# Gathering rows with the one-hot slots as weights, two tiles' choices interleaved, and a shorter untaken branch in a two-layer encoder with a mixture of experts

## The chip, the cores and the metric

The kernel is one program on one core of a Trainium2 chip. The metric is device microseconds of that core for the whole program; lower is better.

## What is computed

The reference is a two-layer encoder over 512 tokens of width 1024 (float32). Each layer is a mixer (attention and recurrences) and then a mixture of experts: every token chooses one of 4 groups, two of the 8 experts in it, and gets the weighted sum of two experts' outputs. Each sub-layer ends in a layer norm. Cut to the part that the change touches:

```python
for i in range(DEPTH):                       # 2
    mix = mixer_i(x, ...)
    x = _layer_norm(ALPHA * x + mix, ln1_g[i], ln1_b[i])
    # mixture of experts
    grp = x @ w_grp + b_grp                  # 4 logits
    exp = (x @ w_exp + b_exp)                # 32 logits
    g_idx = argmax(grp); top_l, top_e = top_k(exp of that group, 2)
    gate = softmax(grp)[g_idx] * softmax(top_l)
    ffn = sum over the two experts e of gate_e * (silu(x @ w_gate[e]) * (x @ w_up[e])) @ w_down[e]
    x = _layer_norm(ALPHA * x + ffn, ln2_g[i], ln2_b[i])
```

The weights of the 32 experts are 201 MB a layer, and all of them are read.

## The kernel before, in words

Tokens lie in 4 tiles of 128 (`NT`). Every expert has 64 slots (`CAP`); two experts make a pair, so 16 pairs of 128 slots. A token's place among an expert's slots is counted by matmuls with a triangle and with ones (`moe_count`); the one-hot matrix `S` (token by slot) is a comparison of that place with 1..64 (`moe_slots`). If an expert has more tokens than slots, a general path (`moe_general`, inside `tc.If(over > 0)`) computes the layer without slots. With this input neither layer takes it, and no row of it is in the trace; the program still loads the flag `rover` on each engine, branches over the path, and lifts the semaphores that the path would have lifted.

`out_rest` is the seam between mixer and experts. For each tile t it finishes the output projection (`out`), adds the residual (`total`), normalizes (`norm`), transposes the tile (`turn`, 8 transposes on TensorE and two copies on ScalarE to `mxT`), computes the 36 logits (`logits`), picks group and experts (`choose`, 13 lines on VectorE that wait each for the one before), counts, places (`place`, which makes `S` for the first pair) and gathers the first pair's rows (`gather`). TensorE and VectorE run this stage in the order in which the code stands. Then come the slots of the second pair for all four tiles, the token numbers of the second pair (`moe_tokens`), the indirect DMA that fetches that pair's rows (`moe_fetch`, issued by GpSimd), two copies of the gathered rows to `xbuf`, and in `moe` the branch and the experts: `up(0, 0)` is the first matmul against expert weights.

In the gather before, the weights of each matmul are a 128 x 128 block of token rows and the 128 slots are the moving operand, so that the result is already transposed as `up` wants it:

```python
for j in range(KJ):          # 8
    self.mm(m["g"][:, j * P:(j + 1) * P], xv[:, j, :], S, ...)
```

Expert weights are loaded by SyncE in blocks of 1 MB (`expect_moe`) to 24 slots of 8 KB a partition (`big`), each as soon as a slot is free. While the seam runs, the slots fill up and no more loads can start until `up(0, 0)` frees the first two.

Of the kernel before, what the change touches and what calls it, by code (L numbers as in the profile page):

```python
# [77 lines left out]
class Kernel:  # L78
# [159 lines left out]
    def setup(self):  # L238
# [209 lines left out]
    def out_rest(self, pool, gbuf, m):  # L448
# [11 lines left out]
        def half_room():  # L460
# [7 lines left out]
            self.nc.gpsimd.memset(m["xr"], 0.0)  # L468
# [44 lines left out]
        def choose(t):  # L513
            self.moe_choose(m, pool, t, ps[t][1])
# [19 lines left out]
        with self.tc.manual_schedule(engines={mybir.EngineType.PE, mybir.EngineType.DVE}):  # L534
# [27 lines left out]
            choose(2)  # L562
            turn(3)
# [453 lines left out]
    def moe_choose(self, m, r, t, pl):  # L1017
# [3 lines left out]
        nc.vector.tensor_tensor(lg, pl, m["br"], op=OP.add)  # L1021
# [6 lines left out]
        def first_hot(o, v, mx, k, op):  # L1028

            fm = r.tile([P, 1], F32, name="fm", bufs=8)  # L1030
            nc.vector.tensor_reduce(mx, v, axis=AX.X, op=OP.max)
            nc.vector.scalar_tensor_tensor(o, v, mx, wt[:, 0:k], op0=OP.is_equal, op1=OP.mult, accum_out=fm)
            nc.vector.tensor_scalar(o, o, 2.0, fm, op0=OP.mult, op1=op)

        first_hot(og, lg[:, 0:4], m["gmx"][:, t:t + 1], NG, OP.is_le)

        nc.vector.scalar_tensor_tensor(grid(s), og[:, :, None].to_broadcast([P, NG, EPG]), -3.0e38, grid(lg[:, 4:36]), op0=OP.mult, op1=OP.add)
        A0, A1 = m["A0"][:, t, :], m["A1"][:, t, :]
        first_hot(A0, s, m["m12"][:, 0, t:t + 1], NE, OP.is_gt)
# [882 lines left out]
```

## Time and profile before

| | us |
|---|---|
| median of 3 runs (1594.83 to 1597.14) | 1596.24 |
| the profiled execution | 1594.33 |
| its span from first to last instruction | 1592.2 |
| TensorE busy in it | 1513.1 |
| VectorE busy | 692.0 |
| ScalarE busy | 440.2 |
| GpSimd busy | 188.0 |
| mean DMA rate | 292 GB/s |

The layers' seams lie at about 305 to 350 us and 1063 to 1107 us, the experts after them to about 815 and 1565 us. Rows from the trace give a start and a length in us from the span's start; PE is TensorE, PEld its weight loads, DVE VectorE, ACT ScalarE, POOL GpSimd, SP SyncE. A "q" behind an engine's name is its sequencer, which runs branches and waits.

### The profile page before, as it was taken

How to read it: one execution, taken by the hardware profiler on the slowest of the kernel's cores; microseconds unless marked ns; L12 is line 12 of the kernel's file. 1: busy time of each engine (PE TensorE's matmuls, PEld its weight loads, DVE VectorE, ACT ScalarE, POOL GpSimd, SP SyncE). 2: the span in 40 equal slices, each digit the busy share in tenths (PEclk: the TensorE clock that was granted, in tenths of full speed). 3: DMA queues.
4: the chain of work that ended last, by engine and by line, in shares of the span. 5: the costliest groups of instructions: out<-in, count | busy, mean ns of one | idle time of the engine just before them, and what ended most of it. 6: DMA issues, size and time to landing. Idle time of an engine off the chain costs nothing. (4 is left out here: it accounts for less than half of the span.)

```text
span 1592.2 us, 19865 instructions
## 1 busy us (share of the span) xinstructions
PE 1513.1 (95%) x7905; PEld 915.1 (57%) x7905; DVE 692.0 (43%) x1215; ACT 440.2 (28%) x770; POOL 188.0 (12%) x278
## 2 busy tenths in 40 slices
PE   7999999979999999999999899998999999999997
PEld 7888788764444444443358787677444444444333
DVE  4655655543334343343445544364333434333334
ACT  4455522012211211211235434511221121111122
POOL 3322211211000000010022200120000000001001
PEclk9999999979999999999999999997999999999999
DMA  8311133749999999999962120385999999999993
GB/s 236 107 54 54 54 133 106 298 164 398 421 419 419 421 421 419 420 420 421 419 246 94 54 75 32 123 338 186 396 420 420 419 421 421 419 419 420 421 420 137
DMA packets 106844, 465.20 MB, mean 292 GB/s; under 512 B 12972, under 2 KB 48268, under 8 KB 57456
## 3 DMA queue, kind: packets, MB, share of 16 engines
q1 hardware_dynamic: 98848, 444.86, 69.8%
q0 software_dynamic: 6160, 12.62, 2.3%
q10 hardware_dynamic: 1728, 6.29, 1.0%
q8 instruction: 67, 1.10, 0.3%
q14 instruction: 41, 0.34, 0.1%
HBM read 462.11 MB, written 9.44 MB: 296 GB/s over the span
## 5 line engine op out<-in xcount | busy, mean ns | idle before, releaser
L213 PE MATMUL pa<-big 128*64 128x512 f32 (+3 forms) x4168 | 838.6, 461 | 18.1 <-DMA big<-in_moe_w_up_dram 7.2
L213 PEld LDWEIGHTS pa<-big 128*128 128x128 f32 (+1 forms) x4168 | 453.0, 166 | 329.9 <-issue 278.5
L213 PE MATMUL pa<-big,hs 128*64 128x512 f32 x992 | 224.9, 592 | 0.0
L1205 DVE SCALAR_TENSOR_TENSOR big<-pa,rgate,big 64x512 fp32r<-64x512 f32 x120 | 90.0, 750 | 213.4 <-ACT big L1204 213.2
L213 PE MATMUL pb<-big 128*128 128x512 f32 (+2 forms) x640 | 173.9, 418 | 6.3 <-DVE big L1160 4.1
L1160 DVE SCALAR_TENSOR_TENSOR big<-big,pb 128x1024 f32<-128x1024 f32 x112 | 134.3, 1220 | 80.0 <-PE pb L213 79.7
L213 PEld LDWEIGHTS pa<-big,hs 128*64 128x64 f32 x992 | 72.6, 137 | 141.0 <-issue 136.1
L213 PEld LDWEIGHTS pb<-big 128*128 128x128 f32 x640 | 122.7, 217 | 51.0 <-issue 26.0
L1204 ACT ACTIVATE big<-pa,rgate 64x512 fp32r<-64x512 f32 x120 | 81.8, 682 | 219.0 <-PE pa L213 170.3
L1175 DVE TENSOR_TENSOR h<-pa,h 64x512 f32<-64x512 f32 x64 | 44.4, 694 | 216.2 <-ACT h L1174 216.2
L1174 ACT ACTIVATE h<-pa 64x512 f32<-64x512 f32 x64 | 37.6, 588 | 260.8 <-PE pa L213 260.8
L203 DVE TENSOR_TENSOR big<-big 128x2048 fp32r<-128x2048 f32 (+2 forms) x38 | 77.0, 2025 | 67.2 <-ACT big L203 49.5
L203 ACT CAST big<-big 128x2048 fp32r<-128x2048 f32 (+2 forms) x39 | 64.7, 1665 | 57.2 <-PE pa L213 23.1
L1139 POOL DMA_INDIRECT big<-x1d,ridx x30 | 31.7, 1058 | 368.4 <-DVE ridx L1113 255.8
L1148 ACT COPY big<-pb 128x1024 f32<-128x1024 f32 x30 | 30.4, 1012 | 127.7 <-PE pb L218 127.7
L1138 POOL MEMSET big<- 128x1024 f32 x28 | 26.6, 952 | 311.8 <-PE pb L218 311.7
L218 PEld LDWEIGHTS pa<-eye,h 64*128 64x128 f32 x256 | 35.4, 209 | 37.8 <-DVE big L1205 23.5
L213 PE MATMUL pb<-big,C 128*128 128x512 f32 x192 | 53.9, 412 | 2.5 <-DVE big L1160 2.5
L218 PE MATMUL pb<-eye,big 128*128 128x128 f32 x288 | 42.6, 288 | 12.4 <-DMA big<-in_x_dram 5.9
L218 PEld LDWEIGHTS pb<-eye,big 128*128 128x128 f32 x288 | 37.3, 195 | 18.5 <-issue 7.5
L1185 DVE COPY hs<-pa 128x256 f32<-128x256 f32 x64 | 27.0, 422 | 44.8 <-PE pa L218 44.7
L213 PEld LDWEIGHTS pb<-big,C 128*128 128x128 f32 x192 | 33.3, 188 | 19.4 <-issue 9.7
(312 smaller groups left out, 1200.5 us busy)
## 6 DMA issues: line engine op xcount, KB each, us to landing
big<-in_moe_w_gate_dram SPq DMA_DIRECT2D x128, 1024.0 KB, 19.8
big<-in_moe_w_up_dram SPq DMA_DIRECT2D x128, 1024.0 KB, 19.8
big<-in_moe_w_down_dram SPq DMA_DIRECT2D x128, 1024.0 KB, 19.8
big<-in_ev_w_in_dram SPq DMA_DIRECT2D x24, 512.0 KB, 5.6
big<-in_od_w_in_dram SPq DMA_DIRECT2D x7, 1024.0 KB, 6.8
big<-in_x_dram SPq DMA_DIRECT2D x8, 512.0 KB, 4.3
big<-in_ev_w_out_dram SPq DMA_DIRECT2D x4, 1024.0 KB, 4.9
x1d<-big ACTq DMA_DIRECT2D x8, 512.0 KB, 7.0
```

The lines of the kernel that those rows point to most:

```text
L203: ins = self.nc.scalar.copy(hi, src), (sub or self.nc.vector).tensor_tensor(lo, src, hi.bitcast(F32), op=OP.subtract)
L213: return self.nc.tensor.matmul(o, a, b, start=start, stop=stop, skip_group_check=True)
L218: self.nc.tensor.transpose(o, a, self.eye[s, s])
L1138: self.nc.gpsimd.memset(x, 0.0)
L1139: self.nc.gpsimd.indirect_dma_start(x, None, self.x1d[:, :], bass.IndirectOffsetOnAxis(m["idx"][:, pair:pair + 1], 0), bounds_check=T - 1, ...
L1148: self.nc.scalar.copy(xn, ps.rearrange("p (j n) -> p j n", j=KJ))
L1160: self.nc.vector.scalar_tensor_tensor(x, x, ALPHA if first else 1.0, ps, op0=OP.mult, op1=OP.add)
L1174: self.nc.scalar.activation(h, o[0:64], AF.Silu)
L1175: self.nc.vector.tensor_tensor(h, o[64:128], h, op=OP.mult)
L1185: self.nc.vector.tensor_copy(hs.rearrange("p j n -> p (j n)"), ps[:, 0:4 * CAP])
L1204: last = self.nc.scalar.activation(hi, src, AF.Copy, scale=g[a:a + 64])
L1205: self.nc.vector.scalar_tensor_tensor(yl[a:a + 64, s], src, g[a:a + 64], hi.bitcast(F32), op0=OP.mult, op1=OP.subtract)
```

## The change

- The gather uses `S` as weights and the token rows as moving operand: 2 matmuls of 512 columns a tile in place of 8 of 128. The result lies slot by feature, so after the branch two copies (one on ScalarE, one on VectorE) bring it to `xr` and `moe_features` transposes it (8 transposes, two copies).
- `choose(1, 2)` interleaves the 13 lines of two tiles. Its place, and those of `turn`, `logits` and `gather`, move.
- `place` makes the slots of both first pairs at once (256 columns); the token numbers and the fetch of pair 1 move behind the branch.
- `turn` writes all 8 transposes before its two copies; `mxT` gets a third buffer.
- `moe_general` is one loop over tiles in place of four copies of a loop body.
- A filler of 160 bytes a partition moves what is allocated behind it: in the built program every `big` slot starts 96 bytes past a multiple of 256 before, and at a multiple of 256 after.

```diff
+        c.tile([P, 40], F32, name="pad")
...
-            self.nc.gpsimd.memset(m["xr"], 0.0)
+            self.nc.gpsimd.memset(self.moe_fetched(m, 1), 0.0)
...
-            xT[t] = pool.tile([P, D], F32, name="mxT", bufs=2).rearrange("p (j n) -> p j n", j=KJ)
+            xT[t] = pool.tile([P, D], F32, name="mxT", bufs=3).rearrange("p (j n) -> p j n", j=KJ)
...
-        def choose(t):
-            self.moe_choose(m, pool, t, ps[t][1])
+        def choose(*ts):
+            for steps in zip(*[self.moe_choose(m, pool, t, ps[t][1]) for t in ts]):
+                for f in steps:
+                    f()
...
-            xv = res[t].rearrange("p (k j) -> p j k", j=KJ)
             S = m["S"][:, t, 0:2].bitcast(F32).rearrange("p e n -> p (e n)")
-            for j in range(KJ):
-                self.mm(m["g"][:, j * P:(j + 1) * P], xv[:, j, :], S, t == 0 and j % 4 == 0, t == NT - 1)
+            for hf in range(2):
+                s = slice(hf * 512, (hf + 1) * 512)
+                self.mm(m["g"][:, s], S, res[t][:, s], t == 0, t == NT - 1)
...
+            count(0)
             st = total(3)
+            place(0)
             logits(1)
-            count(0)
-            place(0)
             norm(3, st)
             turn(2)
-            choose(1)
+            gather(0)
             logits(2)
+            turn(3)
+            choose(1, 2)
             count(1)
             place(1)
-            gather(0)
-            choose(2)
-            turn(3)
+            logits(3)
             gather(1)
             count(2)
             place(2)
-            logits(3)
+            choose(3)
             gather(2)
-            choose(3)
             count(3)
-            pc = self.moe_fit(m)
-            place(3)
+            place(3, 1)
+            self.moe_fit(m)
             gather(3)
-            self.moe_fits(m, pc)
-            for t in range(NT):
-                self.moe_slots(m, t, 1)
-            z = self.pa()
-            self.moe_tokens(m, m["S"][:, :, 2:4], self.idr, z, 1)
-            self.rel(z)
-            self.moe_fetch(m, 1, False)
-            for a in range(2):
-                s = slice(a * 512, (a + 1) * 512)
-                nc.scalar.copy(m["xbuf"][:, s], m["g"][:, s])
-            self.rel(m.pop("g"))
+            self.moe_slots(m, 3, 2, 2)
...
-        for a in range(2):
-            pv = halves[a].rearrange("p (j n) -> p j n", j=4)
-            for j in range(4):
-                self.tr(pv[:, j, :], xv[:, 4 * a + j, :])
-            self.nc.scalar.copy(xT[:, 4 * a:4 * a + 4, :], pv)
+        pv = [h.rearrange("p (j n) -> p j n", j=4) for h in halves]
+        for j in range(KJ):
+            self.tr(pv[j // 4][:, j % 4, :], xv[:, j, :])
+        for a in range(2):
+            self.nc.scalar.copy(xT[:, 4 * a:4 * a + 4, :], pv[a])
...
-        self.moe_gates(m)
-        self.spare = 1
         with tc.manual_schedule(engines={mybir.EngineType.PE}):
+            x = self.moe_fetched(m, 0)
+            for hf in range(2):
+                s = slice(hf * 512, (hf + 1) * 512)
+                (nc.scalar.copy, nc.vector.tensor_copy)[hf](x[:, s], m["g"][:, s])
+            self.rel(m.pop("g"))
+            self.moe_features(x, xn[:, 0], 2)
+            ps = self.pa()
+            self.moe_tokens(m, m["S"][:, :, 2:4], self.idr, ps, 1)
+            self.rel(ps)
+            self.moe_fetch(m, 1, False)
+            self.moe_gates(m)
+            self.spare = 1
             up(0, 0)
...
-        for t in range(NT):
-            x = self.residual(m, t)
-            nc.vector.tensor_copy(xt, x.rearrange("p (n j) -> p j n", j=KJ))
+        with tc.For_i(0, NT, 1) as t:
+            nc.sync.dma_start(w[0][:, 0:D], x1[ds(t, 1)].rearrange("o p n -> (o p) n"))
+            nc.sync.dma_start(gt, gd[ds(t, 1)].rearrange("o p e -> (o p) e"))
+            nc.vector.tensor_copy(xt, w[0][:, 0:D].rearrange("p (n j) -> p j n", j=KJ))
```

On TensorE, from the logits of tile 1 to the second gather in layer 0, the order before (`y` holds the router's weights, `rab` the chosen experts, `big` with 128x128 is a gather):

```order
L213 MATMUL pb<-y_106,mxT 128x36 x8
L213 LDWEIGHTS tri
L213 MATMUL pb<-rab,tri 128x32
L218 MATMUL pa<-eye,big 128x128 x8
L213 MATMUL pa<-y_106,mxT 128x36 x8
L213 LDWEIGHTS ones
L213 MATMUL pb<-rab,ones 128x32
L213 MATMUL pb<-big 128x128 x8
```

and after the change from the same place on (`big` with 128x512 x2 is a gather now):

```order
L213 MATMUL pb<-rab,tri 128x32
L213 MATMUL pb<-y_108,mxT 128x36 x8
L218 MATMUL pa<-eye,big 128x128 x8
L213 MATMUL pb<-big 128x512 x2
L213 MATMUL pa<-y_108,mxT 128x36 x8
L218 MATMUL pa<-eye,big 128x128 x8
L213 LDWEIGHTS ones
L213 MATMUL pb<-rab,ones 128x32
```

The count of tile 0 and the first gather moved ahead of the logits of tiles 1 and 2, and the last turn ahead of the count of tile 1, which waits for the interleaved choices.

On TensorE at the end of the seam in layer 0, before (the last gather, the token numbers, the branch, the first expert matmuls):

```order
L213 MATMUL pb<-big 128x128 x8
L213 MATMUL pa<-idr,big 128x2 x4
L1300 TENSOR_LOAD rover
L1301 COMPARE_AND_BRANCH
...
L1301 UNCONDITIONAL_BRANCH x2
L213 MATMUL pa<-big 64x512 x24
```

and after:

```order
L213 MATMUL pb<-big 128x512 x2
L1293 TENSOR_LOAD rover
L1294 COMPARE_AND_BRANCH
...
L1294 UNCONDITIONAL_BRANCH x2
L218 MATMUL pb<-eye,big 128x128 x8
L213 MATMUL pa<-idr,big 128x2 x4
L213 MATMUL pa<-big 64x512 x24
```

Eight transposes and the token numbers now stand between the branch and the first expert matmuls.

On ScalarE in layer 0 the first rows behind the branch were

```order
L1081 ACT_TABLE_LOAD
L1081 ACTIVATE y_106<-y_106 128x16
L1084 ACTIVATE y_106<-y_106 128x4
```

and are now

```order
L1300 ACT_TABLE_LOAD
L1300 COPY big<-pb 128x512
L1072 ACTIVATE y_108<-y_108 128x16
L1075 ACTIVATE y_108<-y_108 128x4
L1141 COPY big<-pb 128x512 x2
```

The load of ScalarE's table stands ahead of the copy of the gathered rows there; in layer 1 that copy stands ahead of the branch and the table load behind it.

## Rows read from the trace of the kernel before

**Rows 1.** The chain of waits that ended last, in order of time: start, length, what.
```profile
1107.18 11.96 PE pa L213 x48
...
1404.31 20.49 DMA big<-in_moe_w_up_dram
```
**Rows 2.** Groups of instructions by shape, TensorE: busy us, mean ns, idle before them by releaser.
```profile
L213 PE MATMUL pa<-big 128*64 128x512 f32 x2048 | 478.8, 602 | 14.5 <-DMA big<-in_moe_w_up_dram 7.2 <-DVEq L1301 4.0 <-DMA big<-in_moe_w_gate_dram 1.8
```
**Rows 3.** TensorE in order of time, layer 0: start, length, instruction, idle before and releaser.
```profile
307.20 0.71 PE L218 MATMUL pb<-eye,big 128*128 128x128 f32 x4 [1.61 <-ACT mxT L1010]
...
325.51 0.19 PE L213 MATMUL pb<-rab,tri 128*128 128x32 bf16 x1 [2.82 <-DVE rab L1042]
325.53 4.17 PE L213 MATMUL pb<-big 128*128 128x128 f32 x16
...
335.01 1.95 PE L213 MATMUL pa<-y,mxT 128*128 128x36 f32 x16
...
341.75 4.11 PE L213 MATMUL pb<-big 128*128 128x128 f32 x16 [0.59 <-DVE big L1057]
...
350.15 13.30 PE L213 MATMUL pa<-big 128*64 128x512 f32 x48 [3.95 <-DVEq L1301]
```
**Rows 4.** Stretches of layer 0: busy time of each engine, granted TensorE clock, DMA share, GB/s.
```profile
325.50:331.50 6.00, 5.99 (x27) 5.99 (x27) 3.16 (x18) 0.64 (x2) 0.00 (x0) 0.50 1.02 423
...
350.10:355.50 5.40, 5.35 (x13) 3.01 (x15) 2.22 (x11) 1.90 (x4) 1.99 (x3) 0.50 0.06 5
```
**Rows 5.** VectorE in order of time, layer 0.
```profile
312.45 0.20 DVE L1021 TENSOR_TENSOR y<-pb,y 128x36 f32<-128x36 f32 x1 [0.63 <-PE pb L213]
...
316.35 1.36 DVE L490 SCALAR_TENSOR_TENSOR big<-big,pa 128x512 f32<-128x512 f32 x2 [0.71 <-PE pa L213]
...
322.27 0.19 DVE L1021 TENSOR_TENSOR y<-pb,y 128x36 f32<-128x36 f32 x1
...
325.26 0.19 DVE L1042 TENSOR_TENSOR rab<-y 128x32 bf16<-128x32 f32 x1
...
342.02 0.15 DVE L1073 TENSOR_SCALAR rkeep<-rkeep 128x1 f32<-128x1 f32 x1
342.09 0.89 DVE L1057 TENSOR_TENSOR big<-io,rpos 128x128 fp32r<-128x128 f32 x4
```
**Rows 6.** TensorE in order of time, layer 1.
```profile
1072.40 4.56 PE L213 MATMUL pa<-big 128*128 128x512 f32 x12
...
1100.86 4.17 PE L213 MATMUL pb<-big 128*128 128x128 f32 x16 [0.59 <-DVE big L1057]
1104.69 0.99 PE L213 MATMUL pa<-idr,big 128*128 128x2 f32 x4
```
**Rows 7.** TensorE in order of time, end of layer 0: float32 matmuls of 512 columns.
```profile
827.35 1.02 PE L213 MATMUL pb<-big,eye 128*128 128x512 f32 x2
```
**Rows 8.** Groups by shape from 826.5 to 830.5 us, TensorE.
```profile
L213 PE MATMUL pb<-big,eye 128*128 128x512 f32 x4 | 2.0, 593 | 0.0
```
**Rows 9.** The branch's line, layer 0: duration min/median/max in ns, first and last start.
```profile
L1301 DVEq COMPARE_BRANCH  x1: 72/72/72, 346.9 to 346.9; - x1
...
L1301 DVEq EVENT_SEMAPHORE  x1: 21/21/21, 349.9 to 349.9; - x1
```
**Rows 10.** The branch's line, layer 1.
```profile
L1301 DVEq COMPARE_BRANCH  x1: 56/56/56, 1106.1 to 1106.1; - x1
...
L1301 DVEq EVENT_SEMAPHORE  x1: 21/21/21, 1106.7 to 1106.7; - x1
```
**Rows 11.** ScalarE in order of time, layer 0.
```profile
345.89 1.07 ACT L583 COPY big<-pb 128x512 f32<-128x512 f32 x2 [13.87 <-PE pa L213]
347.07 1.28 ACT L1081 ACT_TABLE_LOAD   x1
```
**Rows 12.** GpSimd in order of time, layer 0.
```profile
346.69 1.13 POOL L1139 DMA_INDIRECT big<-x1d,ridx  x1 [6.19 <-DVE ridx L1113]
```
**Rows 13.** DMA issues, 400 to 700 us: count, KB each, median us to landing.
```profile
big<-x1d,ridx POOLq DMA_INDIRECT x10, 8.4
```

More of the change, by code (lines that the diff above doesn't have):

```diff
@@ L242, in setup @@
         self.x1d = dram.tile([T, D], F32, name="x1d")
+        self.gd = dram.tile([P, NT * NE], F32, name="gd")
         self.eye = c.tile([P, P], F32, name="eye")
@@ L511, in logits, with place @@
             ps[t] = z, z[0][:, 0:36], (z[0][:, 512:D] if len(z) == 1 else z[1])[:, 0:NE]
-        def choose(t):
-            self.moe_choose(m, pool, t, ps[t][1])
+        def choose(*ts):
+            for steps in zip(*[self.moe_choose(m, pool, t, ps[t][1]) for t in ts]):
+                for f in steps:
+                    f()
         def count(t):
             self.moe_count(m, t, ps[t][2])
-        def place(t):
-            self.moe_place(m, t, ps[t][2], 0)
+        def place(t, n=2):
+            self.moe_place(m, t, ps[t][2], 2 * n)
             self.rel(*ps[t][0])
@@ L1030, in first_hot @@
             fm = r.tile([P, 1], F32, name="fm", bufs=8)
[L1031 to L1037, printed above, removed]
-        A0, A1 = m["A0"][:, t, :], m["A1"][:, t, :]
-        first_hot(A0, s, m["m12"][:, 0, t:t + 1], NE, OP.is_gt)
-        nc.vector.scalar_tensor_tensor(s, A0, -3.0e38, s, op0=OP.mult, op1=OP.add)
-        first_hot(A1, s, m["m12"][:, 1, t:t + 1], NE, OP.is_gt)
-        nc.vector.tensor_tensor(m["ab"][:, t, :], A0, A1, op=OP.add)
+            return [lambda: nc.vector.tensor_reduce(mx, v, axis=AX.X, op=OP.max),
+                    lambda: nc.vector.scalar_tensor_tensor(o, v, mx, wt[:, 0:k], op0=OP.is_equal, op1=OP.mult, accum_out=fm),
+                    lambda: nc.vector.tensor_scalar(o, o, 2.0, fm, op0=OP.mult, op1=op)]
+        A0, A1 = m["A0"][:, t, :], m["A1"][:, t, :]
+        return [lambda: nc.vector.tensor_tensor(lg, pl, m["br"], op=OP.add),
+                *first_hot(og, lg[:, 0:4], m["gmx"][:, t:t + 1], NG, OP.is_le),
+                lambda: nc.vector.scalar_tensor_tensor(grid(s), og[:, :, None].to_broadcast([P, NG, EPG]), -3.0e38, grid(lg[:, 4:36]),
+                                                       op0=OP.mult, op1=OP.add),
+                *first_hot(A0, s, m["m12"][:, 0, t:t + 1], NE, OP.is_gt),
+                lambda: nc.vector.scalar_tensor_tensor(s, A0, -3.0e38, s, op0=OP.mult, op1=OP.add),
+                *first_hot(A1, s, m["m12"][:, 1, t:t + 1], NE, OP.is_gt),
+                lambda: nc.vector.tensor_tensor(m["ab"][:, t, :], A0, A1, op=OP.add)]
     def moe_count(self, m, t, o):
@@ L1049, in moe_count, with moe_place, moe_slots @@
         self.mm(o, self.tri, ab[:, t, :], t == 0, True)
-    def moe_place(self, m, t, o, pair):
+    def moe_place(self, m, t, o, n):
         self.nc.vector.scalar_tensor_tensor(m["pos"][:, t, :], o, 1.0, m["ab"][:, t, :], op0=OP.add, op1=OP.mult)
-        self.moe_slots(m, t, pair)
-    def moe_slots(self, m, t, pair):
-        self.nc.vector.tensor_tensor(m["S"][:, t, pair % 2 * 2:pair % 2 * 2 + 2], self.io[:, None, :].to_broadcast([P, 2, CAP]),
-                                     m["pos"][:, t, 2 * pair:2 * pair + 2, None].to_broadcast([P, 2, CAP]), op=OP.is_equal)
+        self.moe_slots(m, t, 0, n)
+    def moe_slots(self, m, t, e, n):
+        self.nc.vector.tensor_tensor(m["S"][:, t, e:e + n], self.io[:, None, :].to_broadcast([P, n, CAP]),
+                                     m["pos"][:, t, e:e + n, None].to_broadcast([P, n, CAP]), op=OP.is_equal)
     def moe_fit(self, m):
+        nc = self.nc
         pc = self.pa()
@@ L1147, in moe_features @@
             self.tr(ps[:, j * P:(j + 1) * P], xv[:, j, :])
-        self.nc.scalar.copy(xn, ps.rearrange("p (j n) -> p j n", j=KJ))
+        n = KJ // parts
+        for i in range(parts):
+            self.nc.scalar.copy(xn[:, i * n:(i + 1) * n], ps[:, i * n * P:(i + 1) * n * P].rearrange("p (j n) -> p j n", j=n))
         self.rel(ps)
@@ L1399, in moe_general @@
         acc, h, hT = z[:, 0:D], z[:, D:D + 512], z[:, D + 512:2 * D].rearrange("p (j n) -> p j n", j=4)
-        gc = r.tile([P, 1], F32, name="gen")
-        G = self.moe_weigh(m)
-        for t in range(NT):
-            x = self.residual(m, t)
-            nc.vector.tensor_copy(xt, x.rearrange("p (n j) -> p j n", j=KJ))
+        gc, gt = r.tile([P, 1], F32, name="gen"), r.tile([P, NE], F32, name="gent")
+        nc.sync.dma_start(self.gd, self.moe_weigh(m).rearrange("p t e -> p (t e)"))
+        gd = self.gd.rearrange("p (t e) -> t p e", t=NT)
+        x1, x2 = (d.rearrange("(t p) n -> t p n", p=P) for d in (self.x1d, self.x2d))
+        with tc.For_i(0, NT, 1) as t:
+            nc.sync.dma_start(w[0][:, 0:D], x1[ds(t, 1)].rearrange("o p n -> (o p) n"))
+            nc.sync.dma_start(gt, gd[ds(t, 1)].rearrange("o p e -> (o p) e"))
+            nc.vector.tensor_copy(xt, w[0][:, 0:D].rearrange("p (n j) -> p j n", j=KJ))
             ps = self.pb()
@@ L1435, in moe_general @@
                 nc.vector.scalar_tensor_tensor(acc, po, gc, acc, op0=OP.mult, op1=OP.add)
-                self.rel(pt, po, ph)
-            nc.vector.scalar_tensor_tensor(x, acc, 1.0 / ALPHA, x, op0=OP.mult, op1=OP.add)
+                self.rel(pt, pg, pu, po)
+            nc.sync.dma_start(x2[ds(t, 1)].rearrange("o p n -> (o p) n"), acc)
+        for t in range(NT):
+            a, x = w[t // 2][:, t % 2 * D:(t % 2 + 1) * D], self.residual(m, t)
+            nc.sync.dma_start(a, self.x2d[t * P:(t + 1) * P, :])
+            nc.vector.scalar_tensor_tensor(x, a, 1.0 / ALPHA, x, op0=OP.mult, op1=OP.add)
         for raw, _, _, load in again:
```

11 lines of the change are left out of this document (3 added, 8 removed).

## The prediction

> **What bounds the kernel now.** I read the chain of waits first. In the second expert stage it follows TensorE from its first expert matmuls at 1107.18 us and turns at 1404.31 us to the loads of expert weights [rows 1]; the stage is thus bound by TensorE for some 300 us and then by the weight stream. The groups by shape say how far the two are apart: over both layers the expert matmuls idled 7.2 and 1.8 us for weights, 9.0 us in all, and 4.0 us for a branch [rows 2]. So TensorE is nearly the bound throughout, and the weight stream is just behind it.
>
> Then I asked what starts that stage. The stream rests before it: from 350.1 to 355.5 us the DMA engines are 6% busy [rows 4], because all slots are full and the first are freed by `up(0, 0)`. Call the start of `up(0, 0)` U: 350.15 us in layer 0 [rows 3], 1107.18 us in layer 1 [rows 1]. Whether TensorE or the stream ends the stage, both follow U, so a seam that is shorter by some us shortens the program by as much.
>
> In order of time, TensorE's rows show what fills the seam. It idles 2.82 us for the choice of tile 1, then the four gathers begin, 4.17 us for the first [rows 3]. The clock is at 1.2 GHz (granted 0.50) from 325.5 to 331.5 us, after that idle time, and again from 350.1 to 355.5 us [rows 4]. Call the end of the fourth gather T: 341.75 + 4.11 = 345.86 us, and 1100.86 + 4.17 = 1105.03 us in layer 1 [rows 3, 6]. From T to U there are 4.3 us in layer 0 and 2.15 in layer 1.
>
> **The change part by part.** I rebuild layer 0's seam with the new order.
>
> *Turns.* TensorE's 1.61 us wait between the halves of a turn goes [rows 3]; the logits of tile 0 come that much sooner, but VectorE can start `choose(0)` only 0.63 us sooner, its idle time there [rows 5]. That choice is then late next: 3.18 us long (322.27 to 325.45, as tile 1's), it ends at 315.0, where `total(3)` starts in place of 316.35. Worth 1.35 us.
>
> *Gather.* No row has these operands. The nearest shape is a float32 matmul of 512 columns with full weights: two last 1.02 us, one 593 ns, so one starts 0.43 us after the other [rows 7, 8]. A gather is four such instructions, 1.75 us at 2.4 GHz and, with 512 columns streaming at half speed, 3.4 us at 1.2 GHz, in place of about 4.1. I keep both ends.
>
> *Interleaved choices.* Dependent steps stand a full step apart (13 lines in 3.18 us), independent ones as little as 0.07 us: 342.02 to 342.09 [rows 5]. Two tiles then take between 3.3 us (the second all hidden) and 6.4 (nothing hidden). I take 3.9, since the steps are short and only the accumulator reads add up. But the pair must wait for tile 2's logits: `S` of tile 0 at 318.55, gather to 320.3, logits of 1.95 us [rows 3] to 322.2; the pair ends at 326.1, later than the 325.45 of now.
>
> *The rest of the seam at 2.4 GHz.* Count and logits of tile 3 to 328.1, second gather to 329.85, count and place 0.75, `choose(3)` 3.2 to 333.8 with the third gather hidden under it, count and place 0.8, fourth gather 1.75: T = 336.4, 9.5 us sooner. At 1.2 GHz the second and fourth gathers cost 1.7 each more, and the third outlasts `choose(3)` by 0.4: T = 340.1, 5.7 us sooner.
>
> *From T to U.* New on TensorE: 8 transposes, 1.2 us by the 0.71 for four [rows 3] or 1.9 at 1.2 GHz, and the token numbers, up to 0.99 [rows 6]. TensorE itself is ready 1.5 us after its last matmul (1104.69 + 0.99 = 1105.68 to 1107.18) [rows 1, 6]. In layer 1 the two copies hide in that: U = T + 3.7, or 4.4 at 1.2 GHz, 1.55 to 2.3 more than now. In layer 0 ScalarE's table load, 1.28 us, stands ahead of its copy, half of 1.07 us [rows 11], and VectorE's copy waits for it. From the flag, which is known 1.6 us before T at full clock: 1.1 for the branch, 1.28, 0.54 and 0.64 with two hand-overs of 0.2, so transposes start at T + 2.4 and U = T + 4.3; at 1.2 GHz the table load hides under the gather and U = T + 4.0. Now it is 4.3, so layer 0 loses nothing here.
>
> *Layer 1's T.* Its seam runs like layer 0's 759.1 us later, except that the last 12 output matmuls took 4.56 us there at a fallen clock [rows 6]. Without the idle time in the turn they may keep the clock. That gives 10.3 us sooner at full clock, 5.4 otherwise.
>
> *The shorter general path.* In layer 0 VectorE branched at 346.9 and was through at 349.9; in layer 1 from 1106.1 to 1106.7 [rows 9, 10]. TensorE waits for that. Now VectorE has no token number to wait for and branches under the fourth gather, so I count nothing for the path itself. If its 3.0 us stayed, about 1.4 would show in layer 0 at full clock.
> The Trainium skill ("Runtime: NRT & Kernel Launch", section "Instruction fetch mechanics") says that a taken branch whose target is outside the two blocks of instructions held near the engine stalls for a fetch. The trace agrees in kind: same code, 3.0 us once and 0.6 the other time. By that rule a shorter path makes the stall rarer, which moves the sum only by the 1.4 just named.
>
> *At nothing:* the smaller memset and the third `mxT` buffer. One 1 MB weight load now stands behind the branch on SyncE; it runs while the stream rests anyway [rows 4], and without that cover it costs 2.5 us at 423 GB/s [rows 4]. The slots of pair 1 leave the end of VectorE's list (0.89 us [rows 5]), which is in T to U.
>
> *Sum.* Layer 0: 9.5 - 0 = 9.5 at full clock, 5.7 + 0.3 = 6.0 at the low one. Layer 1: 10.3 - 1.55 = 8.7, or 5.4 - 2.3 = 3.1. Together 18.2 or 9.1. In the new order TensorE idles about 2.9 us before tile 1's count, just where the clock fell before, and again before the fourth gather. So I take three quarters of the way to the low end: 18.2 - 0.75 x 9.1 = 11.4 us. The profiled execution, 1594.3, would become 1582.9; the median of the runs is 1.9 above it, so 1584.8.
>
> **Rivals.**
> (a) *The clock stays at 2.4 GHz*: 18.2 us, 1578. For it: the gathers stream 512 columns rather than reload weights. Against it: the idle time stands where it stood.
> (b) *Aligned slots make the weight stream faster.* The stream's price is known from above: it can give at most the 9.0 us that expert matmuls idled for weights [rows 2]; with the forecast that is 20.4, 1576. Nothing in this trace has another alignment, so no row speaks for or against; the floor is zero.
> The Trainium skill ("DMA: Bandwidth & Descriptors", section "How a descriptor splits into AXI transactions") says that a descriptor that does not start at a multiple of 256 bytes costs extra beats. For 8 KB from 96 that is an estimate of 259 beats in place of 256, 1.2%, and would fill most of that bound. It is stated for what is fetched, and the shifted side here is written, so I give it little.
> (c) *Nothing comes through*: the pair takes 6.4 us, the low clock lasts longer into the experts (half a us for each us of it) or new waits on the copies take the rest. 1593 to 1596.
> (d) *Slower, through the fetch of pair 1.* It was issued at 346.69 [rows 12] and its rows are due after the 48 first expert matmuls, 13.3 us behind U [rows 3], at 363.4. Now the token numbers come at U, some short work on VectorE and GpSimd may precede it (1.5 to 3 us, my estimate), then 1.1 to issue [rows 12], and 8.4 to land when the stream is busy [rows 13]: U + 11 to 12.5, inside by 1 to 2 us. Each us beyond 13.3 is lost in each layer; the change gets slower when a fetch lands later than about U + 19. That needs twice the landing time. A stream that aligned slots slow down by 3% of its last 440 us would do as much.
>
> **How the numbers follow.** Forecast (gain 6 to 16 us) 0.58; (a) 0.12; (b) 0.12; (c) 0.11; (d) 0.07. The range goes from rival (a) with half of (b), 18.2 + 4.5 = 22.7, 1573.5, to a gain of 4, 1592. About 0.2% (3.2 us) is what a measurement of this kernel tells from no change. Faster by more: the first three and a little of (c), 0.84. Within: most of (c), 0.08. Slower: (d) and the rest of (c), 0.08.
>
> **What would show it.** Right: TensorE's expert matmuls start 6 to 9 us sooner in layer 0 and 3 to 9 in layer 1; gathers last 1.8 to 3.5 us; the pair of choices some 3.9; VectorE's branch lies under the fourth gather; the second layer's shift at its end is the sum of both. Wrong: a wait of the pair-1 transposes for a DMA; a granted clock of 0.50 for much longer behind U than 5 us; or idle time for weights that changes by several us, which would be the alignment.

## The result and the profile after

The changed kernel takes 1569.21 us (median of 4 runs, 1568.20 to 1570.60) against 1596.69 us for the kernel before in the same runs: a ratio of 0.9828, 95% interval 0.9811 to 0.9845, 27.5 us less. The forecast was 11.4 us less and its range ended at 1573.5 us. The profiled executions took 1594.33 and 1568.20 us, 26.1 apart; that of the changed kernel has a span of 1566.4 us, 25.8 below that of before.

To see where these 25.8 us came from I mark both traces at four places of a layer: S, the start of the last 24 output matmuls ahead of the seam (299.54 us before, 299.94 after in layer 0); T, the end of the fourth gather; U, the first expert matmul; E, the first `down` matmul of the last expert. TensorE's rows give E in layer 0. Before:

```profile
808.66 3.65 PE L213 MATMUL pb<-big,hs 128*64 128x512 f32 x16
```

and after:

```profile
796.38 3.65 PE L213 MATMUL pb<-big,hs 128*64 128x512 f32 x16
```

| us, layer 0 / layer 1 | before | after | change |
|---|---|---|---|
| S to U (the seam) | 50.61 / 49.41 | 43.74 / 43.04 | -6.87 / -6.37 |
| U to E (the experts) | 458.51 / 457.28 | 452.70 / 450.81 | -5.81 / -6.47 |

The stretch between the layers gave another 0.6 and the one ahead of the first S took 0.4. The seams gave 13.2 us, not far from the forecast of 11.4. The 12.3 us of the expert stages are what it did not have.

TensorE in order of time in layer 0's seam after (start, length, instruction, idle before and its releaser):

```profile
325.88 0.18 PE L213 MATMUL pb<-rab,tri 128*128 128x32 bf16 x1 [2.42 <-DVE rab L1037]
325.91 3.44 PE L213 MATMUL pa<-y,mxT 128*128 128x36 f32 x16
329.15 3.76 PE L213 MATMUL pb<-big 128*128 128x512 f32 x4
...
333.81 1.98 PE L213 MATMUL pb<-big 128*128 128x512 f32 x4 [0.82 <-DVE big L1052]
...
337.76 1.98 PE L213 MATMUL pb<-big 128*128 128x512 f32 x4 [0.58 <-DVE big L1052]
341.87 1.13 PE L218 MATMUL pb<-eye,big 128*128 128x128 f32 x8 [2.12 <-DVE y L1073]
...
343.68 11.97 PE L213 MATMUL pa<-big 128*64 128x512 f32 x48 [0.29 <-ACT big L1141]
```

A gather lasts 1.98 us where it took 4.1 [rows 3], and 3.76 where the clock is low. T is 339.74, U 343.68. The stretches of that seam (busy time by engine, granted clock, DMA share, GB/s) show where that is:

```profile
326.00:332.00 6.00, 6.00 (x21) 4.45 (x21) 0.61 (x2) 0.00 (x0) 0.00 (x0) 0.51 0.84 354
333.00:339.00 6.00, 3.56 (x15) 1.77 (x16) 4.38 (x24) 0.00 (x0) 0.30 (x1) 1.00 0.00 0
343.50:346.50 3.00, 2.82 (x8) 1.18 (x10) 0.89 (x3) 2.20 (x4) 2.82 (x4) 0.50 0.46 149
```

The chain of waits in layer 1's expert stage after, against [rows 1]: TensorE carries it to 1485 us, 397 us behind U where it was 297, and only two loads stand in it.

```profile
1087.93 10.70 PE pa L213 x48
...
1474.63 10.36 PE pa L213 x47
1484.99 19.55 DMA big<-in_moe_w_down_dram
...
1504.60 19.56 DMA big<-in_moe_w_up_dram
...
1524.20 3.65 PE pa L213 x14
```

The expert matmuls' group by shape, against [rows 2] (busy us, mean ns, idle time by releaser), and the weight stream's rate from 400 to 700 us:

```profile
L213 PE MATMUL pa<-big 128*64 128x512 f32 x2048 | 472.7, 599 | 3.6 <-DMA big<-in_moe_w_up_dram 2.9 <-ACT big L1141 0.6
```

```profile
DMA packets 18749, 127.78 MB, mean 426 GB/s; under 512 B 2710, under 2 KB 2710, under 8 KB 3618
```

Idle time for weights fell from 9.0 to 2.9 us, and the stream moves 426 GB/s where the same stretch before had:

```profile
DMA packets 18509, 126.04 MB, mean 420 GB/s; under 512 B 2682, under 2 KB 2682, under 8 KB 3590
```

### The profile page after: what moved, and what is told of

Read it like the earlier page. It is cut to its first block, busy times and chain, and to the rows that moved or that the text cites. A ratio compares the mean times of both kernels' runs of the same rounds, so it can differ in the third digit from the quotient of the medians.

```text
span 1566.4 us, 19698 instructions
## 1 busy us (share of the span) xinstructions
PE 1495.4 (95%) x7825; PEld 892.1 (57%) x7825; DVE 688.4 (44%) x1211; ACT 441.1 (28%) x772; POOL 185.7 (12%) x278
## 5 line engine op out<-in xcount | busy, mean ns | idle before, releaser
L213 PE MATMUL pb<-big 128*128 128x512 f32 (+1 forms) x544 | 160.3, 432 | 9.1 <-DVE big L1153 4.2
L213 PEld LDWEIGHTS pb<-big 128*128 128x128 f32 x544 | 98.0, 190 | 53.4 <-issue 25.2
L1167 ACT ACTIVATE h<-pa 64x512 f32<-64x512 f32 x64 | 37.6, 588 | 264.0 <-PE pa L213 264.0
L1141 ACT COPY big<-pb 128x1024 f32<-128x1024 f32 (+1 forms) x34 | 32.5, 962 | 121.0 <-PE pb L218 121.0
L218 PE MATMUL pb<-eye,big 128*128 128x128 f32 x304 | 43.6, 286 | 10.5 <-DMA big<-in_x_dram 4.9
```

The costliest lines, as they stand in the source:

```text
L213: return self.nc.tensor.matmul(o, a, b, start=start, stop=stop, skip_group_check=True)
L218: self.nc.tensor.transpose(o, a, self.eye[s, s])
L1141: self.nc.scalar.copy(xn[:, i * n:(i + 1) * n], ps[:, i * n * P:(i + 1) * n * P].rearrange("p (j n) -> p j n", j=n))
L1167: self.nc.scalar.activation(h, o[0:64], AF.Silu)
```

## The experiments

Ratios are to the kernel before, run beside each kernel on the same chip, and kernels that ran on different chips are compared by them; the marks are those of above, from one profiled execution each.

| kernel | us | ratio (95%) | S to T | T to U | U to E |
|---|---|---|---|---|---|
| before | 1596.69 | 1 | 46.3 / 47.3 | 4.3 / 2.2 | 458.5 / 457.3 |
| after | 1569.21 | 0.9828 (0.9811 to 0.9845) | 39.8 / 39.6 | 3.9 / 3.5 | 452.7 / 450.8 |
| e1 before, aligned | 1584.49 | 0.9929 (0.9913 to 0.9946) | 46.4 / 45.7 | 4.5 / 1.9 | 452.7 / 452.9 |
| e2 after, unaligned | 1582.40 | 0.9918 (0.9900 to 0.9936) | 40.9 / 39.6 | 3.9 / 3.5 | 458.9 / 455.3 |
| e3 after, at 128 | 1581.72 | 0.9910 (0.9894 to 0.9927) | 40.9 / 39.6 | 3.9 / 3.5 | 459.0 / 456.5 |
| e4 after, at 64 | 1583.53 | 0.9928 (0.9911 to 0.9945) | 40.6 / 39.6 | 3.9 / 3.5 | 457.4 / 456.3 |
| e7 e1 + short path | 1578.26 | 0.9899 (0.9883 to 0.9916) | 46.4 / 45.8 | 0.9 / 1.4 | 452.2 / 452.6 |
| e8 e1 + gather | 1581.43 | 0.9911 (0.9895 to 0.9928) | 42.2 / 42.2 | 6.8 / 7.6 | 453.1 / 452.2 |
| e12 after, long path | 1577.61 | 0.9877 (0.9861 to 0.9893) | 39.6 / 40.0 | 6.8 / 4.8 | 453.2 / 453.1 |
| e11 after again | 1570.00 | 0.9839 (0.9825 to 0.9852) | 40.9 / 39.6 | 3.9 / 3.5 | 453.2 / 450.1 |
| e5 after, filled once | 1567.00 | 0.9828 (0.9811 to 0.9844) | 37.6 / 37.6 | 3.9 / 4.3 | 453.1 / 452.9 |
| e6 after, one by one | 1568.54 | 0.9841 (0.9824 to 0.9857) | 38.4 / 36.6 | 4.8 / 4.1 | 453.0 / 452.3 |
| e9 e6 + filled | 1560.36 | 0.9785 (0.9772 to 0.9799) | 36.1 / 35.9 | 4.9 / 4.3 | 450.3 / 451.0 |
| e10 e9, VectorE copies | 1565.47 | 0.9804 (0.9790 to 0.9817) | 35.5 / 35.5 | 5.0 / 4.7 | 454.0 / 452.7 |
| e16 e9 again | 1562.08 | 0.9791 (0.9778 to 0.9805) | 36.2 / 35.9 | 5.1 / 4.4 | 453.3 / 451.1 |
| e13 e9, load early | 1557.96 | 0.9763 (0.9749 to 0.9776) | 36.0 / 35.5 | 3.9 / 4.1 | 450.4 / 450.7 |
| e14 e13 + e10 | 1559.99 | 0.9777 (0.9763 to 0.9790) | 35.5 / 37.3 | 3.3 / 4.1 | 451.3 / 449.2 |
| e15 after, two turns | 1569.66 | 0.9837 (0.9823 to 0.9850) | 40.8 / 40.7 | 3.9 / 3.5 | 453.1 / 450.2 |

Not every us between two kernels belongs to the edit: ahead of S, where all run the same work, S itself lay anywhere from 297.1 to 301.2 us.

### Is it the alignment of the weight slots?

Theory A: the 160 bytes carry what the prediction missed. Theory B: the stream runs faster because of what the new order leaves behind. e1 gives the kernel before the filler and nothing else; e2 to e4 take it from the changed kernel or give it another size.

```diff
 # e1, kernel before
+        c.tile([P, 40], F32, name="pad")
 # e2, kernel after
-        c.tile([P, 40], F32, name="pad")
 # e3 (slots at 128), e4 (at 64), kernel after
-        c.tile([P, 40], F32, name="pad")
+        c.tile([P, 8], F32, name="pad")     # e4: 56
```

> The kernel before, with nothing but the filler of 160 bytes: every weight slot starts at a multiple of 256 bytes. Theory A (the alignment carries the gain that the prediction missed): the weight stream goes from 420 to 426 GB/s, TensorE's idle time for weights from 9.0 to about 3 us, the seams stay as long as before, and the program gets 7 to 10 us shorter, to about 1587 to 1590 us. Theory B (the stream runs faster because of what the new order leaves behind: fewer instruction fetches, a load moved behind the branch, an earlier start): 420 GB/s and no change, 1596 us.

> The changed kernel without the filler: slots start 96 bytes past a multiple of 256 again, all else as changed. Theory A: the stream is back at 420 GB/s, the seams keep their gain of 6.9 and 6.4 us, and the program takes about 1577 to 1580 us, 8 to 11 slower than the changed kernel. Theory B: 426 GB/s and 1569 us.

> The changed kernel with a filler of 32 bytes: slots start 128 bytes past a multiple of 256. If the multiple that matters is 256, as at 96: 420 GB/s and 1577 to 1580 us. If it is 128 or less: 426 GB/s and 1569 us.

> The changed kernel with a filler of 224 bytes: slots start 64 bytes past a multiple of 256. If the multiple that matters is 64 or less: 426 GB/s and 1569 us. If it is 128 or 256: 420 GB/s and 1577 to 1580 us.

The expert matmuls' group in e1, with the old seam:

```profile
L213 PE MATMUL pa<-big 128*64 128x512 f32 x2048 | 475.0, 601 | 8.3 <-DVEq L1302 5.3 <-DMA big<-in_moe_w_up_dram 2.8
```

and in e2, with the new one:

```profile
L213 PE MATMUL pa<-big 128*64 128x512 f32 x2048 | 475.5, 599 | 11.2 <-DMA big<-in_moe_w_up_dram 8.2 <-DMA big<-in_moe_w_gate_dram 2.3 <-ACT big L1140 0.7
```

The weight idle time goes with the filler alone: 2.8 us with it and the old seam, 10.5 without it and the new one. The rate from 400 to 700 us is 426 GB/s in e1 and 420 in e2, e3 and e4. Theory A holds and B falls. Slots at 64 or 128 past a multiple of 256 bytes are as slow as at 96. Alone the filler is worth 0.71% (11.3 us), more than the 7 to 10 expected; everything else in the change 0.82% (13.1 us), less than expected: e2 to e4 lie 1.7 to 3.5 us above their 1577 to 1580. Both together gave 27.5, which the intervals allow. The filler moves everything that is allocated behind it and not the slots alone, but what changed with it is the rate of the loads, and these go to the slots.

### The parts of the seam

e7 and e8 add one part each to e1, so that the alignment is out of the comparison; e12 takes the short path from the changed kernel.

```diff
 # e7, on e1: moe_general of the changed kernel (one loop over tiles)
-        for t in range(NT):
+        with tc.For_i(0, NT, 1) as t:
 # e12, on after: the reverse
 # e8, on e1
-            for j in range(KJ):
-                self.mm(m["g"][:, j * P:(j + 1) * P], xv[:, j, :], S, ...)
+            for hf in range(2):
+                self.mm(m["g"][:, s], S, res[t][:, s], t == 0, t == NT - 1)
 # e8, ahead of the branch
-                nc.scalar.copy(m["xbuf"][:, s], m["g"][:, s])
+                (nc.scalar.copy, nc.vector.tensor_copy)[hf](x[:, s], m["g"][:, s])
+            self.moe_features(x, m["xbuf"][:, 0:D].rearrange(...))
```

> The kernel before with the filler (1584.5 us) and, besides, the general path as one loop over tiles: less code to branch over, no other change. If the stall of VectorE behind the branch in layer 0 (3.0 us, against 0.6 in layer 1) comes from the length of the code that is jumped: T to U falls from 4.5 to about 2.1 us in layer 0 and stays at 1.9 in layer 1, and the program takes 1581.5 to 1582.5 us. If it comes from elsewhere: 1584 to 1585 us.

> The kernel before with the filler (1584.5 us) and, besides, the slots as weights of the gather (2 matmuls of 512 columns a tile), with the copies, the 8 transposes and their copy ahead of the branch, in the old order and with the old choices. If the gather alone carries most of the seam's gain: each of four gathers goes from 4.1 to 1.9 us, S to T shrinks by 5 to 8 us in a layer, T to U grows by 1 to 3, and the program takes 1574 to 1579 us. If the order and the pair of choices carry it: S to T shrinks by under 3 us and the program takes 1581 to 1587 us.

> The changed kernel with the general path written out four times again, for the tiles one by one. TensorE's branch took 3.4 to 4.8 us over the long path (before, e1, e8) and 0.3 over the short one (e7, the changed kernel). If that wait stands on the path in the new order: T to U grows by 1 to 3 us in each layer and the program takes 1571 to 1575 us. Rival, as the prediction had it (nothing counted for the path): it lies under the fourth gather and the copies, 1569 us.

The branch's row of TensorE's sequencer (ns: least, median, most of the two layers) in the kernel before, which the prediction did not read:

```profile
L1301 PEldq COMPARE_BRANCH  x2: 3528/3654/3781, 343.6 to 1102.6; - x2
```

in the changed kernel:

```profile
L1294 PEldq COMPARE_BRANCH  x2: 313/340/368, 338.6 to 1083.1; - x2
```

in e7:

```profile
L1303 PEldq COMPARE_BRANCH  x2: 228/281/334, 341.3 to 1089.6; - x2
```

in e8:

```profile
L1304 PEldq COMPARE_BRANCH  x2: 4185/4516/4846, 344.4 to 1095.2; - x2
```

and in e12:

```profile
L1294 PEldq COMPARE_BRANCH  x2: 3665/3786/3906, 338.7 to 1088.5; - x2
```

The jump over the long path, which is not run, takes TensorE 3.4 to 4.8 us (3.7 and 3.4 in e1), over the short one 0.2 to 0.4. How much of that shows depends on what runs meanwhile, and on the other engines' branches. In e12 VectorE came through its own branch in layer 0 only at 342.8 us, 4.1 us after it reached it (0.6 in the changed kernel, 338.7 to 339.3), and its half of the copy held up the transposes, though TensorE was past its branch at 342.4. In layer 1 VectorE was through in 0.6 us and its copy early; there TensorE's branch ended last, at 1092.5 (the brackets name another release of VectorE). VectorE's copies and TensorE's transposes, layer 0 and layer 1:

```profile
343.21 0.68 DVE L1300 COPY big<-pb 128x512 f32<-128x512 f32 x1
344.04 1.94 PE L218 MATMUL pb<-eye,big 128*128 128x128 f32 x8 [4.21 <-DVE y L1073]
...
1090.87 0.69 DVE L1300 COPY big<-pb 128x512 f32<-128x512 f32 x1
1092.75 1.24 PE L218 MATMUL pb<-eye,big 128*128 128x128 f32 x8 [2.92 <-DVE y L1077]
```

T to U grew by 2.9 and 1.3 us over e11, and U to E by 3.0 in layer 1, where the clock stood low behind U (the first 48 expert matmuls took 13.55 us, 10.70 in e11). The program took 7.6 us more, which is beyond what was expected; in the profiled executions 2.8 us lie in stretches that the edit does not touch (S is 1.35 us later, the stretch between the layers 1.4 longer). e7 gained 6.2 us on e1 by the medians, 4.8 by the ratios (the two ran on different chips), where 2 to 3 were expected; its seams hold 4.0 of them (50.84 to 47.26 and 47.55 to 47.18), and the profiled S is 3.1 us earlier than e1's. In layer 0 VectorE's stall fell from 3.2 to 0.6 us as expected, and TensorE's branch from 3.7 to 0.2.

e8 is the lesson on the parts' order. The gathers alone shorten S to T by 4.2 and 3.5 us, and T to U takes 2.3 and 5.7 back:

```profile
343.79 1.17 PE L218 MATMUL pb<-eye,big 128*128 128x128 f32 x8 [1.12 <-DVE big L585]
349.12 1.94 PE L213 MATMUL pa<-big 128*64 128x512 f32 x3 [4.16 <-DVE y L1094]
```

The transposes stand ahead of the long branch, so the branch that lay under the fourth gather before now stands bare behind them (TensorE entered it at 344.4 us and left it at 348.6; the bracket names a step of VectorE that ended at about the same time). Neither of the expectation's cases fits it fully: S to T shrank by less than the first case's 5 to 8 us and by more than the second's 3; the time, 1581.43, is the second's. The new gather needs the short path, or the transposes behind it. S to T of the changed kernel is another 2.4 and 2.7 us shorter than e8's; the new order, the turn in one piece and the slots of two pairs at once were not run singly, so what each of them gives is not shown.

### The clock in the seam

```diff
 # e5, on after
             choose(1, 2)
+            for _ in range(3):      # results never read
+                self.mm(ps[2][0][1][:, P:512], self.eye, res[0][:, 0:384], True, True)
             count(1)
 # e6, on after
-            choose(1, 2)
+            choose(1)
             count(1)
             place(1)
+            choose(2)
 # e9, on e6: one such matmul ahead of count(1), gather(2) and count(3),
 # two behind the branch ahead of the transposes
```

> The changed kernel with three extra matmuls of 384 columns (identity as weights, a token tile as moving operand, result never read) on TensorE between the last turn and tile 1's count, where it idles 2.4 us for the pair of choices. They add about 2 us of work in that gap and leave the output as it is. Theory C (the idle time there brings the clock to 1.2 GHz, and the low clock then stretches the logits of tile 3 and the gather of tile 1): the granted clock stays at 1.00 through the seam, T comes 3.3 us sooner in layer 0 and 3.0 in layer 1, and the program takes about 1563 us. Theory D (the clock falls anyway, or the extra matmuls push the count back): 1569 to 1572 us.

> The changed kernel with tile 1 chosen, counted and placed before tile 2's choice starts, in place of the interleaved pair. If interleaving is worth what it saves on VectorE (two choices in 3.35 us in place of 6.4), the third choice starts 1 to 3 us later and the program takes 1571 to 1575 us. Rival: TensorE's idle time before tile 1's count shrinks from 2.4 to about 1 us, the clock stays at 2.4 GHz, and the seam gets some 3 us shorter in each layer: 1562 to 1566 us.

> The changed kernel with choices one by one (as e6) and extra matmuls of 384 columns, results never read, wherever TensorE idles: one before tile 1's count, one before tile 2's gather, one before tile 3's count, two behind the branch before the transposes; the output stays as it is. If the idle time brings the clock down: no stretch at 0.50 between S and U + 3 us, S to T about 36.5 us in both layers, S to U 40 to 40.5 (43.7 and 43.0 in the changed kernel), time 1563 to 1565 us. Rival: the low clock only moves to another place, as in e5; S to U gains 1 to 3 us over both layers, 1566 to 1568 us.

> The changed kernel itself, to stand beside e9, e10 and e12 on one chip: 1567 to 1571 us, S to U 43 to 45 us in layer 0 and 43 in layer 1.

e5, two stretches of layer 0 and one of layer 1:

```profile
325.50:331.50 6.00, 5.18 (x27) 3.26 (x27) 2.59 (x13) 0.00 (x0) 0.00 (x0) 1.00 0.65 274
340.50:342.00 1.50, 1.50 (x6) 0.62 (x4) 0.29 (x1) 1.44 (x2) 1.49 (x2) 0.50 0.08 16
...
1077.50:1086.50 9.00, 7.28 (x23) 4.33 (x23) 2.98 (x13) 4.84 (x8) 2.08 (x2) 0.50 0.42 131
```

With the 2.4 us of idle time filled, TensorE's clock stays at 2.4 GHz where it had fallen, and S to T loses 2.2 and 1.9 us. But the clock falls at other places instead: later, behind the idle times of 0.8, 1.0, 0.6 and 2.1 us that were left, where T to U grows by 0.8 us in layer 1, and in layer 0 also from 315.9 to 319.3 us, ahead of the extra matmuls. The program's ratio is that of the changed kernel: not faster by any measurable amount, against my expectation of 1563.

e6 was to tell what interleaving is worth. Nothing: with tile 1 first, S to T is 1.4 and 3.0 us shorter, although the clock still fell in layer 0 (0.50 from 325.6 to 335.8 us) as it does in the changed kernel. The pair ends its two choices in 3.35 us (322.61 to 325.96) but starts only when tile 2's logits are there; one by one, tile 1's count starts at 324.64 us in place of 325.88. The program is no faster: T to U took 0.9 and 0.6 back (why, the next group shows), and U to E 0.3 and 1.5, as the first 48 expert matmuls of layer 1 stood at the low clock (12.86 us, 10.70 in the changed kernel).

e9 does both and fills the longest gaps. Four stretches of its seam in layer 0:

```profile
317.40:320.80 3.40, 3.35 (x9) 1.92 (x9) 3.18 (x7) 1.17 (x2) 0.54 (x1) 0.50 1.04 437
...
326.00:332.00 6.00, 5.70 (x23) 2.86 (x23) 4.92 (x29) 0.00 (x0) 0.00 (x0) 1.00 0.82 345
333.00:339.00 6.00, 4.81 (x23) 2.58 (x23) 3.07 (x16) 2.08 (x4) 0.13 (x1) 1.00 0.50 156
340.70:343.70 3.00, 3.00 (x14) 1.97 (x16) 0.18 (x1) 1.15 (x1) 2.99 (x4) 1.00 0.35 92
```

The clock is full where it was low in the changed kernel, and in layer 1 from S to behind the first expert matmuls. In layer 0 it still fell once, ahead of the first extra matmul and against the expectation; TensorE had idled 0.79 us at 314 us. In the changed kernel 0.77 us at the same place were not followed by a fall, so what decides it there is not shown. S to T is 36.1 and 35.9 us, and e9 is faster than the changed kernel on the same chip by 9.6 us (1560.36 against 1570.00, intervals apart). Repeated as e16 it took 1562.08.

### What TensorE waits for at U once the seam is short

```diff
 # e10, on e9: no extra matmuls behind the branch, and
-                (nc.scalar.copy, nc.vector.tensor_copy)[hf](x[:, s], m["g"][:, s])
+                nc.vector.tensor_copy(x[:, s], m["g"][:, s])
 # e13, on e9; e15, on after; e14: e10 + this + two extra matmuls behind the branch
-            xT[t] = pool.tile([P, D], F32, name="mxT", bufs=3)...
+            xT[t] = pool.tile([P, D], F32, name="mxT", bufs=2)...
```

> As e9, without the two extra matmuls behind the branch and with both copies of the gathered rows on VectorE, so that neither waits for ScalarE's table load (1.28 us, layer 0) or for its branch. T to U falls from 3.9 and 3.5 us to about 2.6 in both layers: 2 us less than e9, 1561 to 1564 us. Rival: VectorE's branch or gate work ends later than ScalarE's copy did, and T to U stays at 3.5 to 4: as e9.

> As e9, with two buffers of transposed tokens in place of three, which lets the last 1 MB load start before the seam's end and not just ahead of the branch. If TensorE waits at U for that load's landing (1.3 us of idle time in e9): T to U falls from 4.9 and 4.3 us to 3.6 to 3.9 and 3.1 to 3.4, and the program takes 1558 to 1559 us beside 1560 of e9. If it waits for ScalarE's copy: T to U as in e9 and the same time.

> As e10 (both copies on VectorE), with the last load early as in e13 and two extra matmuls behind the branch as in e9. If the load's wait and the low clock behind it were what cost e10 its gain: T to U 2.6 to 3.2 us in both layers, no stretch at 0.50 behind U, 450 to 451 us from U to the last expert's down matmuls, and the program 1556 to 1558 us. Otherwise as e9, 1560, or e10, 1565.

> The changed kernel with two buffers of transposed tokens in place of three; the load that stood behind the branch is issued before the seam's end. By the prediction (that load at nothing, hidden since the stream rests there) the time is the changed kernel's, 1568 to 1571 us. If the load behind the branch costs stream time after U: 1 to 2.5 us sooner in each layer, 1565 to 1567 us. If the third buffer is needed by the order of the turns: later by up to 2 us.

> e9 again, to stand beside e13 and e14 on one chip: 1559 to 1562 us, S to U 40 to 41 us in both layers.

e10 has a shorter S to T than e9 (the clock stayed at 1.00 up to T in both layers) and came out 5 us slower. On SyncE the last load is issued at

```profile
335.88 0.34 SPq L291 DMA_DIRECT2D big<-in_moe_w_gate_dram  x1
```

just ahead of the branch (336.28 us), and TensorE in order of time has

```profile
338.96 0.58 PE L213 MATMUL pa<-idr,big 128*128 128x2 f32 x4
341.58 3.88 PE L213 MATMUL pa<-big 128*64 128x512 f32 x8 [2.04 <-SPq L1301]
```

with the clock behind it

```profile
342.00:346.50 4.50, 4.50 (x12) 2.37 (x11) 0.00 (x0) 0.01 (x1) 2.45 (x4) 0.50 0.50 99
```

The semaphore that SyncE lifts behind the untaken branch is the one that this load lifts when it lands (number 118 in the trace, for both). SyncE passed it at 341.43 us, 5.6 us after the issue (e9 has the same wait, 335.05 to 340.52, with 1.3 us idle before U and the clock kept), and the first expert matmul, whose own data were there (ScalarE's copy ended at 340.31), started at 341.58. Behind that idle time the clock fell, the first 48 expert matmuls took 13.5 us where e9 had 10.7, and U to E grew by 3.7 us in layer 0: the stream starts again only when these matmuls free the first slots.

e13 lets that load start earlier. The wait is gone in layer 0:

```profile
339.69 6.83 PE L213 MATMUL pa<-big 128*64 128x512 f32 x30 [0.33 <-ACT big L1148]
```

T to U falls from 5.1 us (e16, same chip) to 3.9, and the program from 1562.08 to 1557.96, the fastest of all (the intervals of e13 and e16 lie just apart; those of e13 and e9, the same kernel as e16, overlap). In layer 1, TensorE still waits 0.99 us behind SyncE's branch for another load that stands there, and T to U stays at 4.1 where 3.1 to 3.4 were expected. e14 reached 3.3 us from T to U in layer 0 and missed its 1556 to 1558 by 2 us: in layer 1 the clock fell earlier, at 1067 us, and S to T became 37.3. Whether VectorE's copies gain anything beside e13 stays open. e15 gives the changed kernel the early load: 1569.66, the same as e11's 1570.00, as the prediction had it; with U at 343.7 us the load was never awaited.

## Why the prediction was wrong

**The step that failed** is the price of the alignment in rival (b): it stood at nothing in the sum, and its ceiling, "it can give at most the 9.0 us that expert matmuls idled for weights", went into the range by half. Alone it gave 11.3 us (e1), and the sign that the prediction named for it came: idle time for weights fell from 9.0 to 2.9 us. Behind the ceiling stands the reading "TensorE is nearly the bound throughout, and the weight stream is just behind it". In the trace of before the stream has no gap: the DMA engines' busy share is 1.01 to 1.02 in every 24 us from 374 to 782 us. The stage followed the stream: 458.51 / 452.70 is 1.013 and 457.28 / 450.81 is 1.014, and 426 / 420 is 1.014. TensorE's idle time was a bad ceiling, because a wait costs more than the view counts. In the kernel before:

```profile
734.41 5.34 PE L213 MATMUL pa<-big 128*64 128x512 f32 x14 [1.99 <-DMA big<-in_moe_w_up_dram]
...
1472.87 1.02 PE L213 MATMUL pa<-big 128*64 128x512 f32 x2
1474.07 3.65 PE L213 MATMUL pa<-big 128*64 128x512 f32 x14 [0.18 <-DMA big<-in_moe_w_up_dram]
```

The third matmul of the last two rows starts 1.20 us after the first, where two take 0.43 us (16 are 3.44 us apart, 1469.43 to 1472.87): 0.77 us are lost, and 0.18 stand as idle, since the row of two counts as busy for 1.02 us, 0.59 more than two take when others follow (the drain of the pipeline). In the first row the clock fell behind the wait, and 14 matmuls took 5.34 us in place of 3.65. The 12.3 us of the stages are then: 6.1 of idle time, 1.7 of that clock, 2.6 of the first 48 matmuls behind U (13.30 to 11.97 and 11.96 to 10.70), and 1.9 left, for which the drains of the 7 waits that went (9 to 2) are an explanation, not a measurement: at 0.59 us each they would make 4.1. The 2.6 us are not the filler's but the new seam's, by the clock at U: e2, without the filler, has 2.3 of them and e1 none. The filler's own share is clearest in e1, with the old seam: U to E lost 10.2 us there, and 11.5 behind the first 48 matmuls, more than the 9.0. With e1's 11.3 us in the sum the forecast would have been 22.7; the seams gave 1.8 more than their 11.4, and the first 48 matmuls 2.6.

The Trainium skill's rule ("DMA: Bandwidth & Descriptors", section "How a descriptor splits into AXI transactions") was the one thing that spoke for this, with an estimate of 1.2% by its beats. I set it aside because it is stated for what is fetched. The runs show 1.4%, on the side that is written, so they agree in kind; they do not bear out the beats, by which (again an estimate) the loss would be 0.8% at 64 and 1.6% at 128: the rate is 420 GB/s at all three offsets.

**The seam**, step by step. *Gather*: 1.75 and 3.4 us were taken, 1.98 and 3.76 measured (one starts 1.8 us after the other when they follow). *Pair of choices*: 3.9 taken, 3.35 measured; it ended at 325.96, forecast 326.1. The size was nearly right; whether the pair is worth anything was not asked, and e6 shows that one by one S to T is shorter. *T in layer 0*: 336.4 or 340.1 forecast, 339.74 measured, with S 0.4 later. That it came near the low end is in part luck: the clock was low for the logits of tile 3 (3.44 us, where both ends had 1.95) and for the second gather, and full for the fourth, which the low end had at 1.2 GHz. *T to U*: 4.3 forecast for a fourth gather at full clock, as it was, 4.0 at the low one, and 3.94 measured; in layer 1 3.7 to 4.4, and 3.49. *Layer 1's T*: 5.4 to 10.3 sooner, and S to T is 7.7 shorter. Rival (a)'s full clock from S to T came in no run of this order, but in e10, in layer 0 of e14 and in layer 1 of e9, e13 and e16, with extra matmuls and one choice after the other; S to T is 35.5 to 35.9 us there, and the forecast of T = 336.4 is 36.9 behind S.

**The shorter path** was counted at nothing, with "about 1.4" if VectorE's stall stayed. e12 puts it at 2.9 and 1.3 us of T to U. In layer 0 it is the stall that the step names, VectorE's, and longer than before (4.1 us for 3.0), so that its end lay 3.0 us behind T and the fourth gather did not cover it. In layer 1 it is one that the step did not look for: it took VectorE's rows [rows 9, 10] alone, and TensorE's branch, 3.5 to 3.8 us in both layers of before, lay for the most part under the fourth gather and did not show as a wait. The sum came out right since the rebuilt seam takes both engines to be through in time, as they are over the short path; the saving was inside T to U and not seen as the path's. The rule of the Trainium skill on taken branches ("Runtime: NRT & Kernel Launch", section "Instruction fetch mechanics") agrees in kind (the jump over a path that is not run is a taken one): over the long path TensorE stalled in both layers of before, e1, e8 and e12, over the short one in neither layer of e7 and of the changed kernel; which blocks were held, no run shows.

**Counted at nothing and so measured**: the third buffer and the load behind the branch (e15). **Rival (d)** did not come: the fetch was issued at

```profile
344.19 1.13 POOL L1130 DMA_INDIRECT big<-x1d,ridx  x1 [0.17 <-DVE y L1091]
```

0.5 us behind U, and landed 3.6 us later, not 8.4, as the stream rests there; no transpose waited for it.

## What to carry to other kernels

Where a stream of loads runs without a gap, price a faster stream by the stage's whole length, up to where the engine behind it becomes the bound; the engine's idle time alone is no ceiling: a wait also costs the drain of the pipeline and, here, the clock. Put the slots that large loads are written to at multiples of 256 bytes and look whether any small tile ahead of them has shifted them. Before a stage is shortened, list what lies hidden under it on every engine's sequencer, branches and the semaphores behind them above all: here branches of some 4 us, then a load's landing came out one after the other as the cover went.

## What the runs showed of the hardware

- A stream of loads that write 8 KB a partition ran at 420 GB/s where each write starts 64, 96 or 128 bytes past a multiple of 256, and at 426 where it starts at a multiple.
- TensorE's branch over the long path took 3.4 to 4.8 us and over the short one 0.2 to 0.4, though neither path was run; VectorE's 0.6 to 4.1 us over the long one and 0.6 over the short one.
- With matmuls whose results are never read, the granted clock stayed at 1.00 through the seam in layer 1 of e9 and e13, and in layer 0 but for 3.4 us; in the changed kernel, e5 and e6, idle times of 0.6 to 2.4 us had been followed by stretches at 0.50 of 3 to 10 us. S to T lost 0.7 to 2.3 us by them (e5 against the changed kernel, e9 against e6).
- SyncE's semaphore behind an untaken branch waited for a load in flight (5.6 us after its issue), and TensorE waited for SyncE though it did not need that load: in the changed kernel the same load was issued behind the branch at 340.12 us, landed 4.9 us later, and U was 343.68.
